# Where the modulation sums' weights and the rotary tables are made in a two-layer decoder trunk

## The chip, the cores and the metric

The kernel runs on one core of a Trainium2 chip. The metric is the device time of one execution in microseconds (us), given as the median of several runs. A core has TensorE (PE, the matrix multiplier, fed with weights by PEld), VectorE (DVE), ScalarE (ACT), GpSimd (POOL) and SyncE (SP). Each engine works through its own instructions in order; DMAs are issued from SP's and POOL's queues.

## What is computed

A trunk of two layers on 1024 tokens of width 1024, in float32:

```python
def reference(x, c, positions, ada_w, ada_b, norm_g, a_w_in, ...):
    cond = jax.nn.silu(c)
    cos, sin = rope_tables(positions)
    for l in range(DEPTH):
        ada = cond @ ada_w[l] + ada_b[l]
        sh1, sc1, g1, sh2, sc2, g2 = jnp.split(ada, 6, axis=-1)
        h = modulate(rmsnorm(x, norm_g[l, 0]), sh1, sc1)
        ...   # layer 0: mLSTM mixer; layer 1: latent attention on a shared K/V
        x = x + g1[:, None, :] * rmsnorm(y, norm_g[l, 1])
        h = modulate(rmsnorm(x, norm_g[l, 2]), sh2, sc2)
        y = sqrelu_mlp(h, mlp_w1[l], mlp_w2[l])
        x = x + g2[:, None, :] * rmsnorm(y, norm_g[l, 3])
    return x
```

Two things beside the large products matter here. The **modulation**: `cond @ ada_w[l]` is a vector times a 1024 x 6144 matrix for each layer, and `cond @ kv_ada_w` (1024 x 2048) one more for the shared K/V. The **rotary tables**: cosine and sine of position times 32 frequencies, for 1024 positions. They are needed only in layer 1.

```python
def rope_tables(positions):
    inv = ROPE_THETA ** (-jnp.arange(half, dtype=jnp.float32) / half)
    ang = positions.astype(jnp.float32)[..., None] * inv
    return jnp.cos(ang), jnp.sin(ang)
```

## The kernel before

**Products.** Every operand of a product is split into a high part (a cast on ACT, L238) and a low part (a subtraction on DVE, L239), and a product is three matmuls, L280 to L282. `wload` loads 512 KB of weights through SP (L260) into a buffer `raw`, of which there are four, and `wsplit` writes the two parts into two buffers `ws`, of which there are eight. Other buffers: 24 `k4` and eight `hd` of 128 x 1024 floats, six `tmc` and three `tmp` of 128 x 512, one `tma`.

**Halves and stages.** The tokens are worked in two halves of 512. In layer 0 each half goes through the gates (`gates_in`, `gates0`, L689 on: a chain of some twenty DVE and ACT instructions on eight partitions, whose results TensorE turns at L743), q, k and v, the weights within chunks (`intra0`), the chunks themselves (`chunks0`), the output gates (`og0`) and the output projection (`wout`). `split_o` (L797 to L801) multiplies the mixer's output by its gates and splits it. The MLP of layer 0 is then done in three sweeps, the first on the first half and the second on the second half with products of sums of blocks. In the second sweep a step loads a pair of 512 KB tiles (L1020), adds and subtracts them (L1026 to L1028), splits them (L1030, L1031, L238, L239) and stores one combination.

**Modulation.** `ada_chunk` makes 512 columns of a modulation vector: four loads of 512 KB (L377) into `raw`, eight multiply-adds on DVE into `tma` (L382, L384), and a transposition and a sum later on (L364, L366). The chunks are a generator, of which a step is taken here and there beside the products. In the first two sweeps what is left of them runs, and then `latent_weights`: six tiles of layer 1's latent weights are loaded into `raw` (L1563), summed with the shift on DVE (L1567, L1569), scaled on ACT (L1573), split with `wsplit`, and stored (L1578, L1580).

**Rotary tables.** `rope_tables` is drained as a whole ahead of the first gates. It runs on POOL on three `hd` buffers: a conversion, two scalings, seven reductions by parts of 2 pi (two instructions each, L2535 and L2536), a clamp; then two DVE instructions (L2539, L2540), two sines on ACT (L2541, L2542) and two stores. A sine needs another activation table than the exponentials around it.

**Order.** The program is written as generators that are woven by hand, but the final order of each engine's instructions is made by a planner, which runs over the whole program with modelled costs, takes ready instructions by priority (the order of the text, with those under `prompt` or `high_priority` 300 places earlier) and hands out the buffers. `paced` holds DVE instructions behind a given one. The start of the kernel is pinned in the order of the text.

Of the kernel before, what the change touches and what calls it, by code (L numbers as in the profile page):

```python
# [17 lines left out]
P = 128  # L18
# [64 lines left out]
def kernel(  # L83
# [286 lines left out]
    late = [False]  # L370

    def ada_chunk(w, c0, bias, dst):

        acc = tma()
        for q in range(4):
            r = raw().rearrange("p (a b) -> p a b", b=512)
            nc.sync.dma_start(r, wcols(w, c0, 512, 2 * q, 2))  # L377
            for kk in range(2):
                k = 2 * q + kk
                with paced():  # L380
                    if k == 0:
                        nc.vector.tensor_scalar(acc, r[:, kk], cond[:, 0:1], None, ALU.mult)  # L382
                    else:
                        nc.vector.scalar_tensor_tensor(  # L384
                            acc, r[:, kk], cond[:, k : k + 1], acc, ALU.mult, ALU.add
                        )
# [221 lines left out]
    def gates_in(hf):  # L608
# [6 lines left out]
        nc.gpsimd.memset(v7[:, :, 128:VE], 1.0)  # L615
        for t in range(4):
            v = k4()[:, : 7 * VE].rearrange("p (h e) -> p h e", e=VE)
            nc.gpsimd.memset(v[:, :, 128:VE], 1.0)
# [6 lines left out]
        nc.gpsimd.memset(g[:, :, :, 8:32], 0.0)  # L625
# [63 lines left out]
    def gates0(hf):  # L689
# [40 lines left out]
        nc.gpsimd.memset(RM.bitcast(F32), 0.0)  # L730
# [822 lines left out]
    def latent_weights():  # L1553
# [4 lines left out]
        for b, vs in enumerate(views):  # L1558
            A, sh = (Akv, kvada[:, 0:8]) if b < 3 else (Aq, adac(1, SH1))
            r_ = raw()  # L1560
            r = r_.rearrange("p (a b) -> p a b", b=P)
            for c0, v in vs:
                nc.sync.dma_start(r[:, :, c0 : c0 + v.shape[2]], v)  # L1563
            yield
            acc = tma()[:, :P]
            with paced():
                nc.vector.tensor_scalar(acc, r[:, 0], sh[:, 0:1], None, ALU.mult)  # L1567
                for k in range(1, KD):
                    nc.vector.scalar_tensor_tensor(  # L1569
                        acc, r[:, k], sh[:, k : k + 1], acc, ALU.mult, ALU.add  # L1570
                    )
            for k in range(KD):
                nc.scalar.activation(r[:, k], r[:, k], AF.Identity, scale=A[:, k : k + 1])  # L1573
            for i, t in enumerate(wsplit(r_, D)):
# [941 lines left out]
    def rope_tables():  # L2516
# [7 lines left out]
        d, a, kf = hd(), hd(), hd()  # L2524
        pi = d.bitcast(I32)
        nc.gpsimd.tensor_copy(d[:, 0:1], adac(0, SH1)[:, 7:8])
        nc.gpsimd.dma_start(pi, positions.to_broadcast([P, S]))
        nc.gpsimd.tensor_copy(a, pi)
        nc.gpsimd.tensor_scalar(a, a, inv, None, ALU.mult)
        yield  # L2530
        nc.gpsimd.tensor_scalar(kf, a, 1.0 / (2.0 * PI), MAGIC, ALU.mult, ALU.add)
        nc.gpsimd.tensor_scalar_add(kf, kf, -MAGIC)
        for part in TWO_PI_PARTS:
            yield
            nc.gpsimd.tensor_scalar(d, kf, -part, None, ALU.mult)  # L2535
            nc.gpsimd.tensor_add(a, a, d)  # L2536
        yield
        nc.gpsimd.tensor_scalar(a, a, 3.1415925, -3.1415925, ALU.min, ALU.max)
# [377 lines left out]
```

## Time and profile before

| | |
|---|---|
| median of 3 runs | 2339.2 us (2337.68 to 2341.8) |
| the profiled execution | 2336.3 us |
| its span, first to last instruction | 2334.1 us |
| PE busy | 2283.2 us, 98% |
| DVE busy | 1704.7 us, 73% |
| ACT busy | 1126.0 us, 48% |
| POOL busy | 146.3 us, 6% |
| read from and written to HBM | 343.65 and 98.57 MB, 189 GB/s over the span |

All that follows is read from one execution. In a view of waits a row has who waited (engine, tile, line), for whom, the total in us, how often, and the longest. In a view of stretches a row has the stretch and its length, the busy time of PE, PEld, DVE, ACT and POOL with the number of instructions, the clock that was granted to TensorE (1.00 is full), the mean busy share of the 16 DMA engines and GB/s. A row of the timeline begins with start and duration in us, and may end with the idle time before it and what ended it. Rows of groups give busy us and the mean ns of one.

### The profile page before, as it was taken

To read this page: it belongs to the slowest core of one execution; us is meant where nothing else is said; L and a number is where in the kernel's file an instruction comes from. 1 tells how busy PE (TensorE), PEld (TensorE's weight loads), DVE (VectorE), ACT (ScalarE), POOL (GpSimd) and SP (SyncE) were. 2 spreads that over 40 slices of the span, in tenths; PEclk is the share of its full clock that TensorE was granted. 3 is DMA by queue.
4 is the path that set the end of the run, shared out by engine and by line. 5 is a ranking of instruction groups with operands and counts; after the bars stand their busy time and mean duration, and the time that the engine had idled before them with its cause. 6 is when DMAs were issued, how large, how long until landed. Compare 5 with 4: busy or idle time off the path is not lost.

```text
span 2334.1 us, 32606 instructions
## 1 busy us (share of the span) xinstructions
PE 2283.2 (98%) x12042; PEld 1922.5 (82%) x12042; DVE 1704.7 (73%) x2749; ACT 1126.0 (48%) x1911; POOL 146.3 (6%) x231
## 2 busy tenths in 40 slices
PE   8899999999999999999999999999999999999998
PEld 6788798888877778778888778888888888989997
DVE  6776776879778777678774687765666488798776
ACT  4275334665335355544454464444444444655543
POOL 2700000000112220000000000000000000000000
PEclk9999999999999999999999999999999999999999
DMA  9452464657899888566686754874434452455432
GB/s 328 142 166 82 146 198 139 197 185 230 292 291 296 276 292 301 173 216 213 215 266 188 239 181 149 262 249 136 145 100 136 118 167 81 147 156 166 133 109 109
DMA packets 401103, 444.37 MB, mean 190 GB/s; under 512 B 26579, under 2 KB 288784, under 8 KB 400944
## 3 DMA queue, kind: packets, MB, share of 16 engines
q1 hardware_dynamic: 388000, 397.09, 53.7%
q0 software_dynamic: 12944, 45.20, 5.4%
q8 instruction: 95, 1.56, 0.3%
q14 instruction: 64, 0.52, 0.1%
HBM read 343.65 MB, written 98.57 MB: 189 GB/s over the span
## 4 chain that ended last, share of the span: by engine, by line
PE 77%; DVE 9%; DMA 8%; ACT 2%; issue 2%; SPq 1%; DVEq 0%; ACTq 0%
PE ps L280 13%; PE ps L282 12%; PE ps L281 12%; PE pm L280 9%; PE pm L281 9%; PE pm L282 8%; DMA raw<-in_mlp_w_dram 5%; PE pc L281 2%; PE pc L282 2%; PE pc L280 2%; DVE wl L239 1%; DMA raw<-in_a_w_in_dram 1%; PE pc L1969 1%; DVE k L247 1%; PE pm L1774 1%
## 5 line engine op out<-in xcount | busy, mean ns | idle before, releaser
L239 DVE TENSOR_TENSOR wl<-raw,wh 128x1024 fp32r<-128x1024 f32 (+5 forms) x323 | 382.6, 1187 | 210.2 <-ACT wh L238 185.3
L238 ACT CAST wh<-raw 128x1024 fp32r<-128x1024 f32 (+5 forms) x323 | 327.3, 1017 | 421.0 <-PE ps L281 164.7
L280 PE MATMUL ps<-k,wh 128*128 128x512 f32 (+1 forms) x1252 | 475.7, 380 | 5.6 <-DVE tmp L247 2.8
L282 PE MATMUL ps<-k,wl 128*128 128x512 f32 (+1 forms) x1252 | 467.9, 374 | 0.3 <-DVE wl L239 0.3
L281 PE MATMUL ps<-k,wh 128*128 128x512 f32 (+1 forms) x1252 | 467.7, 374 | 0.1
L280 PEld LDWEIGHTS ps<-k,wh 128*128 128x128 f32 x1252 | 235.9, 188 | 51.6 <-DVE tmp L247 3.6
L282 PEld LDWEIGHTS ps<-k,wl 128*128 128x128 f32 x1252 | 235.8, 188 | 42.9 <-DVE wl L239 0.9
L281 PEld LDWEIGHTS ps<-k,wh 128*128 128x128 f32 x1252 | 236.0, 188 | 41.9 <-issue 1.4
L247 DVE TENSOR_TENSOR k<-k,pm 128x512 f32<-128x512 f32 (+1 forms) x250 | 192.4, 801 | 62.7 <-PE pm L282 62.1
L280 PE MATMUL pm<-wh,hd 128*128 128x512 f32 x488 | 193.4, 396 | 2.6 <-ACT raw L1780 1.5
L282 PE MATMUL pm<-wh,hd 128*128 128x512 f32 x488 | 190.4, 390 | 0.0
L281 PE MATMUL pm<-wl,hd 128*128 128x512 f32 x488 | 190.4, 390 | 0.0
L384 DVE SCALAR_TENSOR_TENSOR tma<-raw,cond,tma 128x512 f32<-128x512 f32 x168 | 126.9, 755 | 23.3 <-DMA raw<-in_ada_w_dram 14.2
L280 PEld LDWEIGHTS pm<-wh,hd 128*128 128x128 f32 x488 | 91.7, 188 | 24.1 <-ACT raw L1780 4.0
L282 PEld LDWEIGHTS pm<-wh,hd 128*128 128x128 f32 x488 | 91.6, 188 | 19.9 <-DVE hd L494 0.5
L281 PEld LDWEIGHTS pm<-wl,hd 128*128 128x128 f32 x488 | 91.8, 188 | 18.4 <-issue 0.5
L281 PE MATMUL pm<-hd,wk 128*128 128x512 f32 x256 | 100.0, 391 | 1.7 <-DVE hd L494 1.7
L280 PE MATMUL pm<-hd,wk 128*128 128x512 f32 x256 | 100.8, 394 | 0.6 <-ACT hd L493 0.6
L1780 ACT ACTIVATE raw<-pm,sm 128x128 f32<-128x128 f32 (+3 forms) x64 | 47.5, 743 | 110.8 <-DVE sm L1779 107.2
L280 PE MATMUL pm<-hd,wh 128*128 128x512 f32 x256 | 99.5, 390 | 0.9 <-DVE tma L384 0.9
L282 PE MATMUL pm<-hd,wl 128*128 128x512 f32 x256 | 99.7, 390 | 0.5 <-DVE wl L239 0.5
L282 PE MATMUL pm<-hd,wk 128*128 128x512 f32 x256 | 99.8, 390 | 0.0
(494 smaller groups left out, 4857.5 us busy)
## 6 DMA issues: line engine op xcount, KB each, us to landing
raw<-in_mlp_w_dram SPq DMA_DIRECT2D x176, 512.0 KB, 4.6
raw<-in_ada_w_dram SPq DMA_DIRECT2D x80, 512.0 KB, 4.8
raw<-in_mlp_w_dram SPq DMA_DIRECT2D x128, 256.0 KB, 4.6
raw<-in_a_w_in_dram SPq DMA_DIRECT2D x44, 512.0 KB, 4.5
lo<-wl POOLq DMA_DIRECT2D x32, 512.0 KB, 7.0
wk<-lo SPq DMA_DIRECT2D x64, 256.0 KB, 3.8
xs<-k SPq DMA_DIRECT2D x40, 256.0 KB, 4.4
raw<-in_a_w_out_dram SPq DMA_DIRECT2D x16, 512.0 KB, 4.5
```

The source lines that it names most:

```text
L238: nc.scalar.copy(hi[:, :n], r[:, :n])
L239: i = nc.vector.tensor_sub(lo[:, :n], r[:, :n], hi[:, :n].bitcast(F32))
L247: return f(*a, **k)
L280: nc.tensor.matmul(o, lh, rh, start=start, stop=False)
L281: nc.tensor.matmul(o, lh, rl, start=False, stop=False)
L282: pe_last[0] = nc.tensor.matmul(o, ll, rh, start=False, stop=stop)
L384: nc.vector.scalar_tensor_tensor(acc, r[:, kk], cond[:, k : k + 1], acc, ALU.mult, ALU.add)
L1774: nc.tensor.matmul(o[:, :w], qh, kh, start=False, stop=True)
L1780: nc.scalar.activation(pr[:, :n], f, AF.Exp, bias=m, scale=SCALE, accum_out=l)
L1969: nc.tensor.transpose(pt[:, ts(2 * e + i, P)], u.prs[i][:, ts(b + e, P)], ident)
```

## The change

The diff has two parts.

Part 1 moves `rope_tables`. It is no longer drained ahead of the first gates, but taken two steps at a time beside the eight output gates of the second half. Its POOL instructions become DVE instructions, and a reduction by a part of 2 pi is one instruction in place of two. Its buffers are `k4` in place of `hd`. The memsets on POOL in `gates_in` and `gates0` go to DVE too.

Part 2 adds a flag `apart`, which is set while the first two sweeps are woven. With it `ada_chunk` loads each 512 KB as two DMAs of 256 KB into two `tmc` in place of one `raw`. `latent_weights` always loads its tiles into two `tmc`, and splits them in two halves into two `ws`.

```diff
-    late = [False]
+    late, apart = [False], [False]
...
-            r = raw().rearrange("p (a b) -> p a b", b=512)
-            nc.sync.dma_start(r, wcols(w, c0, 512, 2 * q, 2))
+            if apart[0]:
+                r = [tmc(), tmc()]
+                for kk in range(2):
+                    nc.sync.dma_start(r[kk], w[ts(2 * q + kk, P), c0 : c0 + 512])
+            else:
+                r = raw().rearrange("p (a b) -> p a b", b=512)
+                nc.sync.dma_start(r, wcols(w, c0, 512, 2 * q, 2))
+                r = [r[:, 0], r[:, 1]]
...
-        nc.gpsimd.memset(v7[:, :, 128:VE], 1.0)
+        nc.vector.memset(v7[:, :, 128:VE], 1.0)
         for t in range(4):
...
-            nc.gpsimd.memset(v[:, :, 128:VE], 1.0)
+            nc.vector.memset(v[:, :, 128:VE], 1.0)
...
-        nc.gpsimd.memset(g[:, :, :, 8:32], 0.0)
+        nc.vector.memset(g[:, :, :, 8:32], 0.0)
...
-        nc.gpsimd.memset(RM.bitcast(F32), 0.0)
+        nc.vector.memset(RM.bitcast(F32), 0.0)
...
-            r_ = raw()
-            r = r_.rearrange("p (a b) -> p a b", b=P)
+            r = [tmc(), tmc()]
+            cols_ = lambda t: t.rearrange("p (a b) -> p a b", b=P)
             for c0, v in vs:
-                nc.sync.dma_start(r[:, :, c0 : c0 + v.shape[2]], v)
+                for i in range(2):
+                    nc.sync.dma_start(cols_(r[i])[:, :, c0 : c0 + v.shape[2]], v[:, ts(i, 4)])
...
+            of = lambda k: r[k // 4][:, ts(k % 4, P)]
...
             for k in range(KD):
-                nc.scalar.activation(r[:, k], r[:, k], AF.Identity, scale=A[:, k : k + 1])
-            for i, t in enumerate(wsplit(r_, D)):
+                nc.scalar.activation(of(k), of(k), AF.Identity, scale=A[:, k : k + 1])
+            for i in range(2):
+                nc.scalar.copy(hi[:, ts(i, 512)], r[i])
+                nc.vector.tensor_sub(lo[:, ts(i, 512)], r[i], hi[:, ts(i, 512)].bitcast(F32))
+            for i, t in enumerate((hi, lo)):
...
-        d, a, kf = hd(), hd(), hd()
+        d, a, kf = k4()[:,:1024],k4()[:,:1024],k4()[:,:1024]
         pi = d.bitcast(I32)
-        nc.gpsimd.tensor_copy(d[:, 0:1], adac(0, SH1)[:, 7:8])
         nc.gpsimd.dma_start(pi, positions.to_broadcast([P, S]))
-        nc.gpsimd.tensor_copy(a, pi)
-        nc.gpsimd.tensor_scalar(a, a, inv, None, ALU.mult)
+        nc.vector.tensor_copy(a, pi)
+        nc.vector.tensor_scalar(a, a, inv, None, ALU.mult)
...
         for part in TWO_PI_PARTS:
             yield
-            nc.gpsimd.tensor_scalar(d, kf, -part, None, ALU.mult)
-            nc.gpsimd.tensor_add(a, a, d)
+            nc.vector.scalar_tensor_tensor(a, kf, -part, a, ALU.mult, ALU.add)
...
-    drain(rope_tables())
     drain(with_bg(gates_in(hfs[0]), bgs, 1))
...
     so = split_o(hfs[1])
+    tables = rope_tables()
     for k, _ in enumerate(og0(hfs[1], k4v)):
         if k % 2:
             prompt(next)(so)
         next(bgs)
+        for _ in range(2):
+            next(tables, None)
         if k < 7:
             next(p0)
...
+    apart[0] = True
     two_streams(f0, behind(bg_latent(), 5))
+    apart[0] = False
     rope_perm()
```

18 lines of the change are left out of this document (10 added, 8 removed).

## The prediction

> **What bounds the kernel now.** I read the totals of the page first, then the waits of TensorE, then the stretches in which they lie.
>
> ```profile
> span 2334.1 us, 32606 instructions
> PE 2283.2 (98%) x12042; PEld 1922.5 (82%) x12042; DVE 1704.7 (73%) x2749; ACT 1126.0 (48%) x1911; POOL 146.3 (6%) x231
> ```
>
> TensorE (PE) is busy 2283.2 of 2334.1 us, so an edit that leaves its instructions alone can win at most the 50.9 us in which it stands, and the time it runs at a lower clock. Two stretches that the change touches hold a good part of that. This is the longest wait of TensorE from 78 to 142 us (the gates of the first half of the tokens), and the busy times there (columns: PE, weight load, DVE, ACT, POOL, clock, DMA share, GB/s):
>
> ```profile
> PE pc L743 <- DVE tmc L712: 6.1, 1, 6.1
> ...
> 78.00:142.00 64.00, 55.30 (x388) 49.02 (x387) 55.62 (x79) 31.64 (x70) 28.02 (x14) 0.92 0.53 165
> 98.20:105.00 6.80, 6.60 (x42) 6.37 (x42) 6.56 (x11) 0.52 (x1) 4.27 (x3) 0.77 0.00 0
> 105.00:115.00 10.00, 9.06 (x59) 7.61 (x59) 9.04 (x18) 2.97 (x7) 0.00 (x0) 0.83 0.35 102
> ```
>
> TensorE stands 64 - 55.3 = 8.7 us, 6.1 of them in one wait. The clock costs more: 6.8 us at 0.77 and 10 us at 0.83 lose 0.23 x 6.8 + 0.17 x 10 = 3.3 us, of which I count 2.2, since TensorE also stands there. So 10.9 us can be had. The same two views for the first two sweeps of the first MLP:
>
> ```profile
> PE ps L282 <- DVE wv L1031: 3.8, 4, 1.3
> PE ps L280 <- ACT wv L1030: 3.6, 2, 2.1
> PE ps L280 <- DVE tmp L247: 2.8, 2, 2.1
> ...
> 549.00:860.00 311.00, 298.28 (x1305) 241.18 (x1304) 245.32 (x352) 127.57 (x200) 59.96 (x87) 0.99 0.88 283
> 820.00:840.00 20.00, 19.38 (x78) 15.51 (x78) 15.29 (x20) 8.30 (x13) 4.21 (x7) 0.91 0.97 306
> ```
>
> Here TensorE stands 311 - 298.3 = 12.7 us, and 20 us at a clock of 0.91 lose 1.8 more: 14.5 us can be had. The three waits shown, 10.2 us, all lie in sweep 2.
>
> **Part 1a, the tables leave POOL.** The chain of the gates on VectorE (DVE), once beside POOL's tables and once, for the second half of the tokens, with POOL idle:
>
> ```profile
> 82.68 2.60 DVE L696 TENSOR_SCALAR tmc<-tmc,cols 8x512 f32<-8x512 f32 x1
> 88.22 2.76 DVE L704 SCALAR_TENSOR_TENSOR tmc<-tmc,tmc 8x512 f32<-8x512 f32 x1
> 93.17 4.26 DVE L709 TENSOR_TENSOR_SCAN tmc<-ones,tmc 8x128 f32<-8x128 f32 x4
> 98.18 0.47 DVE L715 TENSOR_TENSOR_SCAN tmc<-ones,mcol,tmc 8x128 f32<-8x128 f32 x1
> ...
> 241.88 0.47 DVE L696 TENSOR_SCALAR tmc<-tmc,cols 8x512 f32<-8x512 f32 x1
> 244.76 0.68 DVE L704 SCALAR_TENSOR_TENSOR tmc<-tmc,tmc 8x512 f32<-8x512 f32 x1
> ...
> L2535 POOL TENSOR_SCALAR hd<-hd 128x1024 f32<-128x1024 f32 x7 | 20.8, 2965 | 0.5
> ```
>
> The same instruction on eight partitions takes 0.47 us without POOL and 2.60 us with it, 0.68 and 2.76: it waits for a good part of one POOL instruction (2.97 us). L696 and L704 lose 2.13 + 2.08 = 4.2 us, and the four scans, at the 0.47 us of a lone one, lose 4.26 - 1.88 = 2.4. That makes 6.6 us ahead of L712, for which TensorE waited 6.1 us: without POOL, L712 is done before TensorE asks. The wait goes and with it most of the lowered clock that follows it. POOL's own time is no gain, since nothing waits for it. Late next is the load of the v weights, whose buffers are freed by DVE in the same crowded stretch and which then need a DMA, a cast and a subtraction; so I don't take all of the 10.9 us but **8.5**. Bounds: 4 (only part of the large wait goes) and 10.9.
>
> The memsets that go to DVE are 14 small ones. Each costs the path nothing unless its tile is still held; DVE stands in order, so one that waits holds back the weight splits behind it. With the twelve half-width casts and subtractions of the latents' weights, in place of six whole ones, I put **0.5 us** (0 to 1.5).
>
> **Part 1b, the tables' new place.** What they cost DVE and ACT, and what is there beside the second output gates (395 to 444 us) and behind them:
>
> ```profile
> L2539 DVE SCALAR_TENSOR_TENSOR hd<-hd 128x1024 f32<-128x1024 f32 x1 | 1.2, 1214 | 0.0
> L2540 DVE TENSOR_SCALAR hd<-hd 128x1024 f32<-128x1024 f32 x1 | 0.7, 678 | 0.0
> ...
> L2541 ACT ACT_TABLE_LOAD x1 | 1.3, 1283 | 0.0
> L2541 ACT ACTIVATE hd<-hd 128x1024 f32<-128x1024 f32 x1 | 1.1, 1063 | 0.0
> ...
> 395.00:444.00 49.00, 49.00 (x218) 40.17 (x217) 39.09 (x54) 32.59 (x50) 0.79 (x8) 1.00 0.69 222
> 444.00:480.00 36.00, 36.00 (x159) 29.45 (x158) 25.89 (x34) 20.59 (x31) 0.00 (x0) 1.00 0.51 166
> ...
> 443.53 1.22 DVE L801 TENSOR_TENSOR k<-hd,k 128x1024 fp32r<-128x1024 f32 x1 [0.52 <-ACT k L800]
> ...
> ACT wh L238 <- PE pm L281: 10.1, 5, 3.2
> ```
>
> DVE: the copy, the five one-input passes and the moved one, 7 x 0.68; the seven reductions and the moved one, 8 x 1.21: 14.4 us. ACT: two sines and up to four table loads (it alternates with the gates' exponentials, as it does now with others), 2 x 1.06 + 4 x 1.28 = 7.2 us. DVE has 9.9 us free up to 444 and 10.1 us from there to 480: it fits only if some 5 us slide behind the gates. What slides is what was traced late and has no priority: the tables, and the first residual. Weight splits and the split of the gated output are pushed ahead, and the splits have cover: ACT waits up to 3.2 us for TensorE to free their buffers. Cover is thin in one place: the last split of the output ends at 444.75, when the projection that reads it has begun. I take a loss of **1.0 us**. Bounds: nothing, and 9.3 us: if all 14.4 us go ahead of that split, less the 7 us that DVE stands in front of it, it is 7.4 us late, and a lowered clock after it costs another 1.9 by the 2.2 above. A gain here is excluded, since TensorE stands nowhere in this window. The tables need three of the 24 large buffers where the gated output's split takes eight; those of the gates come free as the split advances, so I count no wait for them. What else is issued (positions, the two stores) goes to POOL's queue, which is empty there.
>
> **Part 2, small buffers.** Now the modulation sums and latents' weights share the four `raw` buffers with the MLP's weights:
>
> ```profile
> SPq L1020 <- DVE wl L239: 46.0, 14, 9.3
> ...
> DVE k L1026 <- DMA raw<-in_mlp_w_dram: 32.7, 14, 4.3
> ...
> 795.79 0.45 SPq L1563 DMA_DIRECT2D raw<-in_b_w_q_a_dram  x1
> ...
> 789.89 0.50 PE L280 MATMUL ps<-k,wv 128*128 128x512 f32 x1 [1.44 <-ACT wv L1030]
> ...
> 820.53 0.50 PE L280 MATMUL ps<-k,wv 128*128 128x512 f32 x1 [2.13 <-ACT wv L1030]
> ...
> 819.88 0.60 ACT L1030 CAST wv<-raw 128x512 fp32r<-128x512 f32 x1
> ...
> 817.18 1.18 ACT L1573 ACTIVATE raw<-raw,mods 128x128 f32<-128x128 f32 x3 [0.90 <-DVE tma L1569]
> ```
>
> SP waits 46.0 us, 14 times, for DVE's splits to free a `raw` before it can issue sweep 2's weight loads (L1020), and DVE then stands 32.7 us until they land. A latents' tile holds one of the four from its load at 795.79 until it is scaled at 817.18, and TensorE's stall of 820.53 follows; that of 789.89 stands one such tile earlier. With four buffers for the weights alone, one of a pair of loads can go a round earlier. But two things remain. The pair's sum reads the second tile, and its buffer still comes free in the same burst of splits; and the row at 817.18 shows the cast behind eight scalings on ACT that wait for DVE's sums, which no buffer changes. So I take about half of the 14.5 us, **7.0**, between 0 and 14.5.
>
> The added waits: each half load waits for a small buffer, and behind it on SP stand the weight loads, as they do today behind waits for `raw`. The issues themselves: 27 loads of the sums and 7 of the latents become 68, each 0.37 us on SP, 12.6 us over 311, hidden behind the 46.0 us that SP waits.
>
> ```profile
> L377 SPq DMA_DIRECT2D raw<-in_ada_w_dram x16: 367/368/442, 603.2 to 676.0; - x16
> L377 SPq DMA_DIRECT2D raw<-in_kv_ada_w_dram x11: 367/368/531, 549.1 to 593.8; - x11
> ...
> L1563 SPq DMA_DIRECT2D raw<-in_kv_w_a_dram x4: 368/1168/2238, 691.6 to 738.2; - x4
> L1563 SPq DMA_DIRECT2D raw<-in_b_w_q_a_dram x3: 447/472/520, 765.5 to 825.1; - x3
> ...
> raw<-in_mlp_w_dram SPq DMA_DIRECT2D x176, 512.0 KB, 4.6
> ...
> raw<-in_mlp_w_dram SPq DMA_DIRECT2D x128, 256.0 KB, 4.6
> ```
>
> **Sum.** -8.5 + 0.5 + 1.0 - 7.0 = -14.0 us. The profiled execution took 2336.3 us, 2.2 above its span; the median of the runs is 2339.2, 2.9 higher. I take the difference from the median: **2325 us**, and 2316 to 2333 for this case alone.
>
> **Rivals.** *Sweeps unchanged*: the second buffer of the pair and the scalings on ACT decide, and part 2 gives nothing: 2339.2 - 7.0 = 2332. For it speaks the row at 817.18; against it that the stalls come with the latents' tiles. Chance 0.17.
>
> *The tables take it back*: 9.3 us lost beside the gates, -8.5 + 0.5 + 9.3 - 7.0 = -5.7: 2333.5. For it DVE's 39.09 of 49 us; against it the priority of the splits. Chance 0.11.
>
> *Slower, the halved loads fill the DMA engines*: both sizes land in 4.6 us in the rows above. The stage moves 311 us x 283 GB/s = 88 MB, some 168 loads of 512 KB, in 0.88 x 311 = 274 us of all engines, 1.63 us each; 37 us are free. If a half takes as long as a whole, 34 more take 55 us, 18 more than is free, and the sweeps become bound by transfers: 2339.2 - 7.0 + 18 = 2350. It costs something from 37 / 34 = 1.1 us for each added load, and more than part 1 gains from 1.3. Against it: the rows of a half are as long as those of a whole (512 columns), so the packets are the same. Chance 0.10. The Trainium skill (DMA: Bandwidth & Descriptors, Bandwidth) speaks for this rival: it wants loads of 1 MiB and more for three quarters of the peak. That smaller loads don't land sooner here (4.6 and 4.6 us) agrees with it.
>
> *All of it* (10.9 + 14.5 with nothing lost): 2314, chance 0.05. The forecast has 0.57.
>
> **How the numbers follow.** About 0.2% (4.7 us) is what a measurement of this kernel can tell from no change, so faster begins below 2334.5. The forecast, the full gain, most of the first rival and half of the second lie there: 0.78. Within 0.2% lie the rest of these: 0.10. Slower: the third rival, and a little for a new order of the instructions, which the planner makes anew for the whole kernel: 0.12. For 8 in 10 the range takes in the forecast's own, the full gain and the first two rivals with some spread: 2311 to 2338.
>
> **What would show it.** Right: L696 and L704 at about 0.5 and 0.7 us in the first gates, no wait for L712, the clock at 1.0 from 98 to 115 us; no standing of TensorE from 395 to 480; fewer waits on L1030, L1031 and L247 in sweep 2, and SP's waits before L1020 shorter. Wrong: waits for L801 or the first residual near 444; stalls in sweep 2 as before beside an early L1020; a DMA share near 1.0 there. The whole would be wrong if the new order opened waits far from the change, after 900 us, where I counted none.

## The result, and the profile after

The changed kernel takes **2322.6 us** (median of 4 runs, 2319.4 to 2324.0), the kernel before 2340.5 us beside it (4 runs, 2337.7 to 2341.8): a ratio of 0.9923, 95% interval 0.9906 to 0.9940. The forecast was 2325, in a range of 2311 to 2338. The profiled execution of the changed kernel took 2324.0 us, 12.3 less than that of before. The medians differ by 17.9, since that execution of before lay 4.2 below its median and this one 1.5 above.

In the changed kernel lines from L384 up to the latents' weights bear numbers 6 higher, those behind it 13 higher: L696, L704, L709, L712, L1020, L1030 and L1031 are now L702, L710, L715, L718, L1026, L1036 and L1037. L377 is L382 where a sum goes through `raw` and L379 where it goes through `tmc`; L1563 is L1570 and L1573 is L1583.

The totals of the page:

```profile
span 2322.2 us, 32704 instructions
...
PE 2280.8 (98%) x12042; PEld 1921.8 (83%) x12042; DVE 1702.5 (73%) x2782; ACT 1129.4 (49%) x1919; POOL 90.7 (4%) x196
```

TensorE now stands 41.4 us in place of 50.9, and ran the same 12042 matmuls in 2.4 us less, at a mean clock of 0.998 in place of 0.996.

**The first gates.** The timeline of DVE, the waits of TensorE from 70 to 145 us (there is no other), and the busy times there (columns as before):

```profile
82.81 0.47 DVE L702 TENSOR_SCALAR tmc<-tmc,cols 8x512 f32<-8x512 f32 x1
...
85.14 0.68 DVE L710 SCALAR_TENSOR_TENSOR tmc<-tmc,tmc 8x512 f32<-8x512 f32 x1
...
87.66 1.36 DVE L715 TENSOR_TENSOR_SCAN tmc<-ones,tmc 8x128 f32<-8x128 f32 x4
```

```profile
PE pc L791 <- ACT tmc L775: 0.5, 1, 0.5
```

```profile
78.00:145.00 67.00, 66.47 (x482) 59.58 (x480) 53.36 (x111) 32.15 (x80) 0.00 (x0) 1.00 0.60 179
98.00:105.00 7.00, 6.54 (x56) 5.66 (x55) 5.58 (x10) 2.25 (x7) 0.00 (x0) 1.00 0.54 154
```

The instructions that took 2.60, 2.76 and 4.26 us take 0.47, 0.68 and 1.36. The wait of 6.1 us is gone, 0.5 us of standing is left of 8.7, and the clock is at 1.00 where it was 0.77.

**The tables' new place.** The reductions on DVE, and the busy times of the second output gates and of what follows:

```profile
L2547 DVE SCALAR_TENSOR_TENSOR k<-k,k x7: 1215/1217/1219, 399.3 to 414.0; 128x1024 f32<-128x1024 f32 x7
```

```profile
392.00:441.00 49.00, 49.00 (x218) 40.22 (x217) 46.37 (x59) 36.02 (x49) 0.55 (x1) 1.00 0.66 211
441.00:480.00 39.00, 39.00 (x172) 31.96 (x171) 32.56 (x43) 28.37 (x40) 1.48 (x10) 1.00 0.64 200
```

DVE is busy 46.4 of 49 us, and TensorE doesn't stand at all, there or up to 480.

**The first two sweeps.** The longest waits of TensorE, the busy times of the same 311 us, and SP's waits ahead of sweep 2's pairs of loads:

```profile
PE ps L280 <- ACT wv L1036: 1.4, 1, 1.4
PE ps L280 <- DVE tmp L247: 1.1, 2, 0.5
PE pc L282 <- DVE wl L239: 1.0, 2, 0.5
```

```profile
549.00:860.00 311.00, 306.72 (x1357) 250.15 (x1356) 253.49 (x368) 135.32 (x215) 63.10 (x96) 1.00 0.89 294
```

```profile
SPq L1026 <- DVE wv L1037: 44.4, 13, 7.3
...
SPq L1026 <- DVE wl L239: 20.3, 12, 5.0
```

TensorE is busy 8.4 us more of the same stretch (306.72 against 298.28), and the rate rose from 283 to 294 GB/s at nearly the same DMA share (0.88, 0.89). SP's two waits were 33.1 and 46.0 us in before.

**What wasn't forecast.** TensorE's waits from 200 to 400 us, the first of them in the timeline, and the busy times behind it:

```profile
PE ps L280 <- ACT wh L238: 1.5, 1, 1.5
PE pc L890 <- DVE tmc L864: 1.1, 1, 1.1
PE ps L282 <- DVE wl L239: 0.5, 1, 0.5
```

```profile
269.75 0.50 PE L280 MATMUL ps<-k,wh 128*128 128x512 f32 x1 [1.49 <-ACT wh L238]
```

```profile
270.00:280.00 10.00, 9.47 (x43) 7.68 (x43) 6.97 (x10) 3.43 (x6) 0.00 (x0) 0.83 0.77 220
271.00:274.00 3.00, 3.00 (x7) 2.42 (x8) 1.87 (x3) 0.09 (x1) 0.00 (x0) 0.50 0.91 273
```

The kernel before had 0.6 us of waits there. The clock of 0.83 is the mean of some three us at half clock (the second row) and the rest at full. This 3.1 us of standing and the lowered clock lie in the second half's gates and chunks, which the prediction didn't price.

To place all this, each kernel's span is cut at seven events that all kernels share: the first turning of the gates by TensorE (L640), the first and the last output-gate exponential of the first half (L682), the first one of the second half, the first store of sweep 1 (L1003), the last of sweep 2 (L1053), and the last load of the latents' weights (L1605; lines of before). In us, with what TensorE stands in brackets where it matters; "again" is e12, a second profiled execution of the changed kernel:

| kernel | start | first gates | outputs 1 | second half | outputs 2 | sweeps | MLP, rest of it | rest | span |
|---|---|---|---|---|---|---|---|---|---|
| before | 72.2 | 83.7 (8.7) | 63.4 | 180.2 (0.6) | 86.8 | 391.6 (12.8) | 530.5 | 925.7 | 2334.1 |
| changed | 72.4 | 72.6 (0.5) | 63.5 | 184.1 (3.1) | 86.8 | 382.2 (4.3) | 534.2 | 926.4 | 2322.2 |
| changed, again | 73.9 | 72.6 (0.5) | 63.5 | 183.7 (2.6) | 86.7 | 380.4 (2.5) | 532.3 | 926.2 | 2319.3 |
| e1_part1 | 75.5 | 72.7 (0.5) | 63.4 | 182.2 (2.6) | 86.8 | 388.5 (11.0) | 534.4 | 929.2 | 2332.7 |
| e2_part2 | 71.9 | 83.5 (9.0) | 63.4 | 180.1 (0.4) | 86.8 | 378.5 (1.6) | 533.4 | 927.1 | 2324.7 |
| e3_halves | 73.9 | 81.2 (6.2) | 63.5 | 178.9 (0) | 86.8 | 385.5 (8.8) | 532.9 | 925.1 | 2327.8 |
| e4_dve_early | 77.7 | 74.7 (5.6) | 63.4 | 181.3 (1.7) | 86.7 | 389.1 (9.8) | 533.0 | 927.8 | 2333.7 |
| e5_null | 73.8 | 81.4 (6.3) | 63.5 | 180.0 (0.4) | 86.8 | 390.4 (12.4) | 532.3 | 927.8 | 2336.0 |
| e6_sums_only | 73.6 | 83.4 (8.3) | 63.5 | 180.3 (0.6) | 86.7 | 385.2 (7.5) | 531.1 | 927.2 | 2331.0 |
| e7_latents_only | 72.7 | 83.3 (8.3) | 63.4 | 180.1 (0.5) | 86.7 | 385.4 (6.0) | 533.1 | 928.2 | 2332.9 |
| e8_pool_late | 73.1 | 72.7 (0.5) | 63.4 | 188.4 (5.6) | 87.3 | 389.4 (11.5) | 532.2 | 928.2 | 2334.7 |
| e9_sums_apart | 74.3 | 72.7 (0.5) | 63.4 | 185.7 (4.5) | 86.7 | 378.6 (1.9) | 532.6 | 926.1 | 2320.1 |
| e10_memsets_pool | 73.5 | 72.4 (0) | 63.5 | 180.9 (1.3) | 86.7 | 377.8 (1.6) | 532.5 | 927.6 | 2314.9 |
| e11_after_null | 73.3 | 72.6 (0.5) | 63.4 | 182.4 (2.8) | 86.8 | 379.7 (3.0) | 532.8 | 924.8 | 2315.8 |

### The profile page after: what moved, and what is told of

Its sections match the earlier page's. It is cut to its first block, busy times and chain, and to the rows that moved or that the text cites. A ratio compares the mean times of both kernels' runs of the same rounds, so it can differ in the third digit from the quotient of the medians.

```text
span 2322.2 us, 32704 instructions
## 1 busy us (share of the span) xinstructions
PE 2280.8 (98%) x12042; PEld 1921.8 (83%) x12042; DVE 1702.5 (73%) x2782; ACT 1129.4 (49%) x1919; POOL 90.7 (4%) x196
## 4 chain that ended last, share of the span: by engine, by line
PE 78%; DMA 8%; DVE 8%; issue 2%; ACT 2%; SPq 1%; POOL 0%; DVEq 0%; ACTq 0%; POOLq 0%
PE ps L280 13%; PE ps L282 13%; PE ps L281 13%; PE pm L280 8%; PE pm L281 8%; PE pm L282 8%; DMA raw<-in_mlp_w_dram 4%; PE pc L281 2%; PE pc L280 2%; PE pc L282 2%; DVE wl L239 1%; DVE k L247 1%; PE pc L1982 1%; DMA raw<-s 1%; PE pm L1787 1%
## 5 line engine op out<-in xcount | busy, mean ns | idle before, releaser
L238 ACT CAST wh<-raw 128x1024 fp32r<-128x1024 f32 (+2 forms) x317 | 321.4, 1016 | 430.5 <-PE ps L281 178.0
L239 DVE TENSOR_TENSOR wl<-raw,wh 128x1024 fp32r<-128x1024 f32 (+2 forms) x317 | 375.0, 1185 | 197.4 <-ACT wh L238 172.8
L281 PEld LDWEIGHTS ps<-k,wh 128*128 128x128 f32 x1252 | 236.6, 189 | 41.4 <-issue 1.4
L281 PEld LDWEIGHTS pm<-wl,hd 128*128 128x128 f32 x488 | 91.8, 188 | 18.3 <-issue 0.5
L390 DVE SCALAR_TENSOR_TENSOR tma<-raw,cond,tma 128x512 f32<-128x512 f32 x120 | 89.5, 746 | 17.6 <-DMA raw<-in_ada_w_dram 8.4
L281 PE MATMUL pm<-hd,wk 128*128 128x512 f32 x256 | 100.1, 391 | 1.7 <-DVE hd L500 1.7
L280 PE MATMUL pm<-hd,wk 128*128 128x512 f32 x256 | 100.9, 394 | 0.6 <-ACT hd L499 0.6
L280 PE MATMUL pm<-hd,wh 128*128 128x512 f32 x256 | 99.5, 390 | 1.1 <-ACT hd L499 0.8
L281 PE MATMUL pm<-hd,wh 128*128 128x512 f32 x256 | 99.7, 390 | 0.2 <-DVE hd L500 0.2
```

The lines of the kernel that those rows point to most:

```text
L238: nc.scalar.copy(hi[:, :n], r[:, :n])
L239: i = nc.vector.tensor_sub(lo[:, :n], r[:, :n], hi[:, :n].bitcast(F32))
L280: nc.tensor.matmul(o, lh, rh, start=start, stop=False)
L281: nc.tensor.matmul(o, lh, rl, start=False, stop=False)
L390: nc.vector.scalar_tensor_tensor(acc, r[kk], cond[:, k : k + 1], acc, ALU.mult, ALU.add)
```

## The experiments

The theory to test was the prediction's own: part 1 gains in the first gates because POOL no longer stretches DVE there, and part 2 gains in the sweeps because background tiles no longer hold the MLP's `raw`. The rivals: the halving of the loads does what the buffers seem to do, or the planner's new order does it.

The programs were also set side by side, engine by engine. Part 2 alone moves no instruction of TensorE and none of any engine ahead of the sweeps, though it does give DVE, ACT and SP a new order within them; part 1 moves instructions of TensorE only ahead of the sweeps. Behind the sweeps no row of TensorE stands elsewhere in the changed kernel. So before, e2, e5, e6 and e7 are five executions of one order up to the sweeps, and the changed kernel, e1, e11 and e12 four of another. Their spread is the measure of what one execution can show: first gates 81.4 to 83.7 and 72.6 to 72.7, second half 180.0 to 180.3 and 182.2 to 184.1.

### Each part alone: e1_part1 and e2_part2

e1 is the changed kernel with the sums and the latents' tiles as before; e2 is the kernel before with them as in the diff.

```diff
 e1, against the changed kernel
-    apart[0] = True
     two_streams(f0, behind(bg_latent(), 5))
-    apart[0] = False
...
-            r = [tmc(), tmc()]
+            r_ = raw()
 e2, against the kernel before
+    apart[0] = True
     two_streams(f0, behind(bg_latent(), 5))
+    apart[0] = False
...
-            r_ = raw()
+            r = [tmc(), tmc()]
```

> Part 1 alone: tables on VectorE beside the second output gates, memsets on VectorE, the modulation sums and latents' weights in the large buffers as before. Theory (POOL slowed VectorE's chain of gates; the sweeps are a matter of buffers): the first output gate's exponential (155.9 us before, 145.0 after) comes at 145.0 +- 0.5, the second output gates (399.5, 392.6) at about 392.6, the first block of sweep 1 (its first store at 486.3, 479.4) at about 479.4, and the two sweeps keep their 391.6 us (first store of sweep 1 to last store of sweep 2; 382.2 after), so that some 7 us of the gain remain: about 2332 to 2334. Rival (a new order made by the planner gives the gain, in whatever part): the stages differ from both kernels, and the sweeps are shorter here too.

> Part 2 alone: the modulation sums and latents' weights through six small buffers in the first two sweeps, tables on POOL at the start as before. Theory (buffers): first output gate at 155.9 +- 0.5 as before, with TensorE's wait of 6.1 us for the gates; from the first store of sweep 1 to the last store of sweep 2 382 +- 2 us in place of 391.6; about 9 us less in all, some 2331. Rival (the parts need each other: the sweeps are faster only because VectorE or POOL come to them less loaded): the sweeps keep more than 388 us.

Measured: e1 2331.3 us (6 runs), ratio 0.9967 (0.9954 to 0.9979); e2 2325.1 us (4 runs), ratio 0.9942 (0.9928 to 0.9957), before 2338.5. The forecast gave each part 7.0 us (-8.5 + 0.5 + 1.0, and -7.0); part 1 has that, and part 2 is the larger: 13.3 us of time against 7.1. The table shows where: e1 has the whole gain of the first gates (83.7 to 72.7) and loses 2.0 in the second half; e2 gains 13.1 us in the sweeps and leaves the stages ahead of them as they were. The numbers of the expectations were missed in places: e1's first output gate came at 148.2 us and not at 145.0, since its start took 75.5 us, and its sweeps took 388.5 and not 391.6; e2's took 378.5, less than the 380 to 384 expected. Both rivals fall: e2's sweeps are short without part 1, and e1's gain lies in the gates, its sweeps being only 1.9 to 3.1 us shorter than in two executions of before (e5 is the other). The waits in e2's sweeps, longest first:

```profile
PE pc L282 <- DVE wl L239: 0.9, 2, 0.5
PE pm L280 <- ACT hd L499: 0.5, 1, 0.5
PE ps L280 <- ACT wv L1036: 0.3, 1, 0.3
```

Of the 10.2 us in the three rows of before, 0.3 is left.

### Halving without the buffers, and a null: e3_halves and e5_null

e3 keeps `raw` and only loads each sum's and each latents' tile as two halves of 256 KB. e5 is the kernel before with one memset that does no work that counts, written at the latents' weights and meant to make the planner order the kernel anew.

```diff
 e3, against the kernel before
-            nc.sync.dma_start(r, wcols(w, c0, 512, 2 * q, 2))
+            for kk in range(2):
+                nc.sync.dma_start(r[:, kk], w[ts(2 * q + kk, P), c0 : c0 + 512])
...
-                nc.sync.dma_start(r[:, :, c0 : c0 + v.shape[2]], v)
+                for i in range(2):
+                    nc.sync.dma_start(r[:, ts(i, 4), c0 : c0 + v.shape[2]], v[:, ts(i, 4)])
 e5, against the kernel before
         Aq = gain(5, NG(1, 0), adac(1, SC1))
+        nc.vector.memset(lbias[:, 0:1], 0.0)
```

> The kernel before with only the loads of the modulation sums (all of them) and of the latents' weights halved: two DMAs of 256 KB (the latents' too) into the same large buffer. Theory (the packets are the same, only the buffers count): the sweeps keep 391.6 +- 2 us, DMA share there 0.88 as before, total 2337 to 2342. Rival of the prediction (a half load costs the engines as much as a whole): the share rises towards 1.0 and the sweeps take 18 us more, about 2355. Other rival (the halving itself brings the gain, since a half lands earlier): the sweeps fall towards 382.

> Control: the kernel before with one superfluous memset of one column on VectorE ahead of the latents' weights. It changes nothing that the prediction speaks of, but the planner orders everything behind it anew. Theory (the gain of part 2 is a matter of buffers, that of the later stages a matter of order): TensorE's standing in the two sweeps stays between 11 and 13 us (12.75 before, 11.0 with part 1 alone), and the later stages (last store of sweep 2 to the end, 1456.2 before, 1458 to 1464 in the other four) come out some us longer than before's, since its order is only one of several. Rival (any new order gives the sweeps' gain): standing below 8 us.

e3 took 2329.6 us in one run; its sweeps 385.5 us, 6.1 less than before. Its waits there and its busy times:

```profile
PE ps L280 <- ACT wv L1031: 4.3, 2, 2.3
PE ps L282 <- DVE wv L1032: 2.7, 4, 1.0
...
549.00:860.00 311.00, 302.20 (x1330) 246.18 (x1329) 248.76 (x357) 131.55 (x206) 62.65 (x90) 0.99 0.89 288
```

So the expectation failed: the sweeps didn't keep their 391.6 us. By this one run halving alone brings about half of part 2's gain, and not where the buffers bring theirs: the waits for the pairs' cast and subtraction (L1031 and L1032, L1030 and L1031 in before) are still 7.0 us. They were 7.4. With the sums alone in small buffers these waits are 3.6 us, with the latents' alone 1.4 (e6 and e7, below), with both 0.3. The rival that a half lands earlier has something for it here: in the sweeps e3's halves of the sums landed in 4.5 and 5.0 us (median, from the two tensors), the whole loads of before in 5.6 and 5.5. Nor do the halves fill the DMA engines: the share is 0.89 against 0.88, at 288 GB/s against 283.

e5 took 2336.5 us (8 runs), ratio 0.9995 (0.9983 to 1.0006). It did not do what it was meant to: the planner put the memset among DVE's first instructions, at 2.2 us of the trace, and left every other row of every engine where it was. So it says nothing of a new order. That rival is answered for TensorE, which e2 doesn't move; for the order of DVE, ACT and SP within the sweeps, which is new in e2, e3, e6 and e7, it stays open. As it is, e5 is a second execution of the kernel before: first gates 81.4 and not 83.7, sweeps 390.4 and not 391.6, and behind the sweeps 1460.1 us in place of 1456.2. The profiled execution of before, on which the prediction was built, was a lucky one at its end.

### Which tiles: e6_sums_only and e7_latents_only

Both on the kernel before: in e6 only the sums go through `tmc`, in e7 only the latents' tiles.

```diff
 e6, against e2
-            r = [tmc(), tmc()]
+            r_ = raw()
 e7, against e2
-    apart[0] = True
     two_streams(f0, behind(bg_latent(), 5))
-    apart[0] = False
```

> The kernel before with the modulation sums alone through halved loads into small buffers in the first two sweeps; the latents' weights stay in a large one. Theory: what stands at the sums' loads (L364, the first product of sweep 2, L247: some 4 us of 12.75) goes, and the latents' rounds keep their stalls on L1030 and L1031 (7.4 us and the lowered clock): standing 7 to 9 us in the sweeps, 385 +- 2 us for them. Rival (all of it is the prefetch of the sums): standing below 4.

> The kernel before with the latents' weights alone through small buffers. Theory: the stalls on the casts and subtractions of sweep 2's weights (7.4 us with a lowered clock) go, those at the sums' loads stay: standing 3 to 6 us in the sweeps, 381 to 385 us. The prediction's doubt (the casts stand behind the scalings on ACT, and no buffer changes that): the stalls on L1030 and L1031 stay, standing 10 or more.

One run each: 2332.8 and 2334.7 us. The sweeps are 6.4 us shorter with the sums alone and 6.2 with the latents alone, 13.1 with both: the two add up. The waits of TensorE in the sweeps and SP's ahead of the pairs, e6 first:

```profile
PE ps L280 <- ACT wv L1036: 2.2, 1, 2.2
...
SPq L1026 <- DVE wl L239: 59.1, 16, 10.6
SPq L1026 <- DVE wv L1037: 39.1, 14, 7.0
```

```profile
PE ps L282 <- DVE wv L1037: 1.4, 2, 1.0
...
SPq L1026 <- DVE wv L1037: 42.7, 12, 7.0
...
SPq L1026 <- DVE wl L239: 15.1, 11, 5.0
```

With the latents out of `raw`, SP waits 57.8 us before the pairs' loads; with them in it 98.2 (before: 46.0 + 33.1). SP's waits alone don't set the time: e6 has more of them than before and shorter sweeps. The wait for the cast L1036 has gone in e7. But the order on ACT has changed with the buffers. In before, from the second of the six tiles on, the cast stands behind all eight scalings of a tile and the tile's own cast (the prediction's rows at 817.18 and 819.88); in e7, as in e2 and the changed kernel, it runs between them:

```profile
808.35 1.56 ACT L1583 ACTIVATE tmc<-tmc,mods 128x128 f32<-128x128 f32 x4 [2.83 <-DVE tma L1575]
...
810.47 0.40 ACT L1583 ACTIVATE tmc<-tmc,mods 128x128 f32<-128x128 f32 x1
810.77 0.60 ACT L1036 CAST wv<-raw 128x512 fp32r<-128x512 f32 x1
...
812.24 0.98 ACT L1583 ACTIVATE tmc<-tmc,mods 128x128 f32<-128x128 f32 x3
```

So e7 doesn't tell the buffers from the order on ACT: either could have taken this stall, and no run holds one of the two still.

### Engine or place: e4_dve_early and e8_pool_late

Both are e1 with one half of part 1 undone. In e4 the tables run on DVE, but ahead of the first gates as before. In e8 they run at the new place, but on POOL.

```diff
 e4, against e1
+    drain(rope_tables())
     drain(with_bg(gates_in(hfs[0]), bgs, 1))
...
-    tables = rope_tables()
...
-        for _ in range(2):
-            next(tables, None)
 e8, against e1 (so for each of the tables' instructions)
-        nc.vector.tensor_scalar(a, a, inv, None, ALU.mult)
+        nc.gpsimd.tensor_scalar(a, a, inv, None, ALU.mult)
...
-            nc.vector.scalar_tensor_tensor(a, kf, -part, a, ALU.mult, ALU.add)
+            nc.gpsimd.tensor_scalar(d, kf, -part, None, ALU.mult)
+            nc.gpsimd.tensor_add(a, a, d)
```

> Part 1 with the tables on VectorE but at their old place, drained ahead of the first gates; part 2 left out. Tells the engine from the place. Theory (what cost TensorE 10.9 us was VectorE being late with the gates, by POOL's contention): 14.4 us of table work on VectorE in the stretch where it is busy 55.6 of 64 us must be done somewhere before 145; the planner can put it behind the gates, so L696 and L704 take about 0.5 and 0.7 us, and the first output gate comes between 145 and 156, nearer 148. Rival (the place alone matters): the first output gate stays at 155 or later, with TensorE waiting for the gates again.

> Part 1 with the tables' instructions still on POOL, at the new place beside the second output gates; part 2 left out, memsets on VectorE. Tells the place from the engine. Theory (POOL slows only what runs beside it, and beside the second output gates the weights are split ahead): the first output gate comes as early as with part 1 (72.7 us behind the first turn of the gates, 83.7 before); VectorE's two-input instructions take longer from 395 to 460 us, and TensorE stands there 0 to 3 us. Rival (contention costs the same wherever it is): TensorE stands 6 us or more there, and the gain of the gates is lost again.

One run each: 2335.5 and 2336.5 us. e8's first gates take 72.7 us, as e1's: to take the tables out of the place is enough, whatever engine they are on. e4's chain has short instructions too, but the tables' stand between them: its first output gate comes at 152.4 us of the span, e1's at 148.2, that of before at 155.9. That is 3.5 of e1's 7.7 us. Against all executions (155.2 to 157.0 in before's order, 145.0 to 148.2 in the new one) it is rather a third. In the table a part of what is lost shows in e4's start, 77.7 us, in which most of the tables' instructions run (from 66.8 us on). So the engine alone is worth a third to a half of the gain, less than the theory's "nearer 148", and the rival's 155 or later didn't come either:

```profile
85.16 0.47 DVE L702 TENSOR_SCALAR tmc<-tmc,cols 8x512 f32<-8x512 f32 x1
85.55 1.20 DVE L2543 SCALAR_TENSOR_TENSOR k<-k 128x1024 f32<-128x1024 f32 x1
...
89.17 0.68 DVE L710 SCALAR_TENSOR_TENSOR tmc<-tmc,tmc 8x512 f32<-8x512 f32 x1
```

e8 then loses elsewhere. Its planner drew most of the tables' work forward from the output gates to the chunks, so that what POOL costs beside the output gates wasn't tested as meant. The busy times of its chunks, the largest of the tables' groups on POOL and the wait there:

```profile
346.00:392.00 46.00, 42.00 (x230) 34.67 (x229) 34.87 (x66) 14.50 (x34) 35.16 (x15) 0.93 0.35 103
```

```profile
L2540 POOL TENSOR_SCALAR k<-k 128x1024 f32<-128x1024 f32 x7 | 20.1, 2866 | 0.6
```

```profile
PE pc L890 <- DVE tmc L864: 4.0, 1, 4.0
```

And the same small instruction of DVE in the chain ahead of L864, in e8 and in e1:

```profile
367.30 2.12 DVE L859 SCALAR_TENSOR_TENSOR sm<-sm 128x4 f32<-128x4 f32 x1
```

```profile
369.19 0.16 DVE L859 SCALAR_TENSOR_TENSOR sm<-sm 128x4 f32<-128x4 f32 x1
```

POOL is busy 35.2 of these 46 us, and TensorE stands 4.0 of them in one wait for DVE, where it waits 0.9 to 1.1 us with the tables on DVE beside the output gates. It is the loss of the first gates once more at another place.

### The second half's loss: e9_sums_apart, e10_memsets_pool, e11_after_null, e12_after_again

These four start from the changed kernel. e9 lets the sums use `tmc` from the second half's gates on; e10 puts the memsets of `gates_in` and `gates0` back on POOL; e11 adds e5's memset, and as there it moved no other row; e12 is the changed kernel unaltered.

```diff
 e9
     drain(gates_in(hfs[1]))
+    apart[0] = True
...
     drain(bg0)
+    apart[0] = False
 e10 (and so for the other three)
-        nc.vector.memset(RM.bitcast(F32), 0.0)
+        nc.gpsimd.memset(RM.bitcast(F32), 0.0)
 e11
+        nc.vector.memset(lbias[:, 0:1], 0.0)
```

> The changed kernel, but the modulation sums load through the small buffers also beside the second half's gates and output (from the second half's gates to its last chunk), where they still go through raw. Theory A: the changed kernel loses 3.9 us there because a sum's tiles hold raw, so that SP stands 20.6 us before the load of the next v weights and TensorE then stands 1.5 us and loses 1.7 us of clock: the stage from the first half's last to the second half's first output-gate exponential falls from 184.1 to 180 to 181 us, SP's wait before L260 for the sums goes from 20.6 us to under 5, and the time is 2318 to 2320. Theory B: the loss comes from DVE alone, which is fuller there since the memsets and the gates' chain moved: the stage stays at 183 to 185 us though SP waits less, and the time stays at 2322. Theory C: six small buffers, which the gates use as well, become scarce there: the gates wait for them and the stage is over 185 us, the time 2325 or more.

> The changed kernel with its fourteen small memsets (the ones of the v tiles, the gates' zeros, RM) back on POOL. Theory A: the memsets cost nothing on either engine: every stage within 0.7 us of the changed kernel, the second half's stage at 184 us, the time 2322. Theory B: the memsets on DVE hold the weight splits back by what I put at 0.5 us, or more: the first gates or the second half's stage are 0.5 to 3 us shorter, 2319 to 2321.5. Theory C: the memsets themselves, beside DVE, are part of what part 1 took away: the first gates are 1 us or more longer than 72.6.

> The changed kernel with one more memset on DVE, of a column that is written again before it is read, placed in the latents' weights: it does no work that counts, but the order of everything behind the first sweep is made anew, while the order ahead of it stays as it is. Theory A: what the changed kernel gives back behind the sweeps (+3.7 and +0.7 us against before) is the luck of an order: the third MLP part and the rest sum to something else by 2 us or more (1460.6 us in the changed kernel, 1456.2 before), while the first gates stay at 72.6 and the second half's stage at 184.1 within 0.7. Theory B: it belongs to the change: the sum stays at 1460 to 1461.5 us. The sweeps stay at 380 to 384 us under both.

> The changed kernel once more, unaltered, on another chip. It has the same instructions in the same order as its first run, and from the first MLP on nearly the order of the kernel with the memsets on POOL, whose sweeps took 377.8 us against 382.2. Theory A: what the memsets on DVE cost in the second half's stage is the same every time: TensorE stands 2.5 to 3.1 us there and waits 1.1 to 1.5 us for the cast L238, the stage takes 182 to 184.5 us (memsets on POOL: 1.25 us, no such wait, 180.9 us); the time is 0.992 to 0.993 of before. Theory B: both are chance of one execution: the standing is under 2 us, the stage 180 to 181.5 us, the time near 0.991 of before as with the memsets on POOL. For the sweeps: if one execution differs from another by some us, this one lies between 378 and 381 us; if the 4.4 us belong to the memsets, at 382 again.

**e9**: 2322.3 us (5 runs), ratio 0.9939 (0.9926 to 0.9953). Theory A is half right. The stall near 270 us and its lowered clock are gone, but the stage is longer, 185.7 us, because another wait has come, for a sum itself. The wait, and the busy times of the ten us in which it lies:

```profile
PE pc L364 <- DVE tma L390: 3.7, 1, 3.7
```

```profile
320.00:330.00 10.00, 6.33 (x29) 5.38 (x28) 7.81 (x22) 1.55 (x4) 0.00 (x0) 0.83 0.30 88
```

So without the sums' hold on `raw` that stall doesn't come, and to free it at this place only moves it: C's number for the stage came true, but not by gates that wait. The hold alone doesn't make the stall, though. SP stands as long there in before, without it (before first, then the changed kernel):

```profile
SPq L260 <- DVE tma L384: 28.3, 6, 20.9
```

```profile
SPq L260 <- DVE tma L390: 29.3, 7, 20.6
```

**e10**: 2317.0 us (4 runs), ratio 0.9912 (0.9898 to 0.9925). The second half takes 180.9 us. Its longest wait of TensorE from 145 to 395 us, and under it the two longest of e12:

```profile
PE pc L890 <- DVE tmc L864: 0.9, 1, 0.9
```

```profile
PE ps L280 <- ACT wh L238: 1.2, 1, 1.2
PE pc L890 <- DVE tmc L864: 0.9, 1, 0.9
```

The wait for the cast L238 is there in the changed kernel's two executions, e1, e4, e8 and e11 (1.1 to 1.5 us each), which have these memsets on DVE and the sums in `raw`. It is absent in e10, which differs from the changed kernel by the memsets alone, and in before, e2, e6 and e7, which have them on POOL. **e12** took 2319.2 us (5 runs), ratio 0.9924 (0.9911 to 0.9938), with the second half at 183.7 us again. So these memsets on DVE cost 1.3 to 3.2 us in this stage: Theory B of e10 and A of e12, at the lower end with the 182.2 and 182.4 us of e1 and e11. The two ends differ by the clock: behind this wait it was lowered in the changed kernel's two executions (0.83 over ten us) and stayed at 1.00 in e1 and e11.

The traces show most of the way from the memsets to the stall. This is the load that the cast waits for, in before, the changed kernel and e10, where the stage begins at 219.3, 208.5 and 209.4 us:

```profile
273.85 0.37 SPq L260 DMA_DIRECT2D raw<-in_a_w_in_dram  x1
```

```profile
264.39 0.37 SPq L260 DMA_DIRECT2D raw<-in_a_w_in_dram  x1
```

```profile
263.92 0.37 SPq L260 DMA_DIRECT2D raw<-in_a_w_in_dram  x1
```

It is issued 54.5 to 54.6 us into the stage in before, e2, e5, e6, e7 and e10, which have the memsets on POOL, and 55.9 to 56.0 us into it in the changed kernel, e1, e4, e8, e11 and e12, which have them on DVE. Its `raw` comes free with a sum on DVE that stands behind the gates' chain, and that chain ends 1.4 us later there. A cast that comes 1.4 us later is a wait of 1.1 to 1.5 us. What delays the chain isn't shown: the fourteen memsets are small (the largest takes 0.48 us), and some of DVE's and TensorE's instructions stand in another order in e10. By the times alone e10 and the changed kernel are not told apart: their intervals overlap.

**e11**: 2317.3 us (4 runs), ratio 0.9919 (0.9904 to 0.9934). Its expectation rested on a new order behind the first sweep, and there was none. So its 1457.6 us behind the sweeps are one more execution of the changed kernel, beside 1460.6 and, in e12, 1458.5. Theory A's 2 us were met by chance of the execution.

e10 has the lowest time of all that ran.

## Why the prediction came out

| step | forecast | first execution | e12 | e11 |
|---|---|---|---|---|
| 1a, the first gates | -8.5 (-4 to -10.9) | -11.1 | -11.1 | -11.1 |
| memsets and half splits (second half) | +0.5 (0 to 1.5) | +3.9 | +3.5 | +2.2 |
| 1b, the tables' place | +1.0 (0 to 9.3) | 0.0 | -0.1 | 0.0 |
| 2, the sweeps | -7.0 (0 to -14.5) | -9.4 | -11.2 | -11.9 |
| behind the sweeps | 0 | +4.4 | +2.3 | +1.4 |
| start and outputs 1 | 0 | +0.3 | +1.8 | +1.1 |
| sum, of the span | -14.0 | -11.9 | -14.8 | -18.3 |

All three are taken against the one execution of before that the prediction used. Against e5 the first column's first gates would be -8.8 and what lies behind the sweeps +0.5.

**1a was right in its mechanism and undersized.** The standing of 8.7 us fell to 0.5 and the clock came back. The forecast kept 2.4 us back for a late load of the v weights behind the wait; no such wait followed in the first gates. By the five executions of before's order (83.1 us in the mean) and the four of the new one (72.6) the gain is 10.5 us, near the bound of 10.9. e8 shows that POOL at this place is the cause, whatever engine the tables run on elsewhere.

**The memsets were mis-sized.** The prediction priced them on the path they stand on, at 0.5 us with a bound of 1.5, and never looked at the second half's gates, where they make a chain late; behind it stands a sum that holds a `raw`, and behind that a load with no margin. By the same nine executions the stage is 3.0 us longer (180.1 to 183.1), of which e10 gives 2.2 back; what is left lies in the wait L890 for L864, 0.9 us in e10 too. This is the one bound that the runs broke. The prediction's last paragraph looked for such a wait only after 900 us.

**1b was right, at its lower bound.** DVE is 46.4 of 49 us busy, the output gates and the projection take 86.8 us in both kernels, and TensorE never stands. ACT loads its tables six times (422.65 to 443.38 us), where the forecast counted four, at 1.28 us each, and that costs nothing either. What slides, as argued, is the tables: their last DVE instruction runs at 437 us. The rival in which they take the gain back has fallen.

**Part 2 was right in sign and undersized, by a doubt that didn't come true.** The forecast took half of 14.5 us, because the second tile's buffer still comes free late and because the cast stands behind eight scalings, "which no buffer changes". e2 gave 13.1 of the 14.5. The order on ACT, which the forecast held fixed, changed with the buffers: from the second tile on, the cast stands behind five to seven scalings in place of all eight. Whether it would have been late behind all eight is open. The rival *sweeps unchanged* has fallen by the times. In the changed kernel's three executions the gain is 9.4, 11.2 and 11.9 us, in e10, with all but the same order there, 13.8. Why one execution keeps 4.3 us of standing where another keeps 1.6 is open. A little of it comes back directly behind the sweeps, as said below.

**The halved loads did not fill the DMA engines.** Each half was priced at a whole load's 1.63 us of all engines. Measured: 34 more loads at shares of 0.89 and 0.90, 294 and 295 GB/s in the changed kernel and e2. The share rose no faster than the rate, so by these, as an estimate, a half took about half as long of the engines as a whole. The forecast compared landings over the whole kernel, of other weights. In the sweeps the sums' loads land in 5.6 and 5.5 us in before, their halves in 5.7 and 5.6 in the changed kernel and in 4.5 and 5.0 in e3. The Trainium skill (DMA: Bandwidth & Descriptors, Bandwidth) wants loads of 1 MiB and more for three quarters of the peak; between 512 and 256 KB, at this share, no run here shows a loss of rate. That agrees with the argument against this rival, that the packets stay the same.

**Behind the sweeps** the forecast had 0. The time of these 1460 us is too uncertain to tell more from it: the 13 other executions took 1457.6 to 1463.6 us, and e5, with none of the change, 1460.1. It is the 1456.2 of the execution used that stands out. But part 2 does cost something there. In the first 30 us behind the last store of sweep 2, in before and the changed kernel:

```profile
877.90:907.90 30.00, 30.00 (x135) 24.82 (x134) 18.89 (x22) 14.87 (x22) 1.59 (x3) 1.00 0.87 324
```

```profile
861.60:891.60 30.00, 28.12 (x122) 22.39 (x121) 18.61 (x22) 13.75 (x20) 1.57 (x3) 1.00 0.89 321
```

TensorE stands there 1.3 to 1.9 us in all seven kernels that have the latents' tiles in `tmc`, and not at all in the seven that have them in `raw`, though its instructions are the same. So of what part 2 wins in the sweeps this much is given back at once.

So the forecast's 2325 came near 2322.6 partly by luck, by errors of both signs: some 2 to 2.6, 1.0 and 2.4 to 4.9 us too little gain in its three large terms, against 2.5 too little loss by the memsets' stage and the 1.3 to 1.9 us behind the sweeps. The parts agree with the whole: by the ratios part 1 alone is worth 7.7 us and part 2 alone 13.6, together 21.3; the changed kernel has 18.0 of it and e10 20.6.

## What to carry to other kernels

When a background stream shares prefetch buffers with the main one, look at the wait of the queue that issues both: a tile that is consumed late holds back every load behind it, and the stall can show far from the tile, as a wait for a cast or a subtraction of a quite different weight. Such an edit may also change the order on the other engines, so look at that before naming the buffer as the cause. Before moving small instructions to another engine, look for every place where they run, not only for the one that the change is about: here fourteen memsets gave back about a fifth of what the tables' move had won. And when a stall goes, the clock that it had lowered comes back too: count both in full unless a named wait stands behind. But the same stall lowers the clock in one execution and not in the next, so take the sum from more than one execution, for a stage far from the change can differ by 4 us by itself.

## What the hardware showed that wasn't expected

- One wait of 1.5 us (changed kernel, 269.75) was followed by some three us at half clock, which makes the ten us from 270 a mean of 0.83; the ten us of e9 that hold its wait of 3.7 us have the same 0.83. The clock costs 0.17 x 10 = 1.7 us, as much as the short stall itself. But it doesn't always fall: behind the same wait (1.1 and 1.4 us) it stayed at 1.00 in e1 and e11.
- How well a stage repeats with the same order depends on the stage: outputs 1 and 2 within 0.1 us, the second half of before within 0.3 and its first gates within 2.3, the changed kernel's sweeps only within 2.5 (382.2, 380.4, 379.7) and its start within 1.5.
- POOL's contention reaches whatever DVE chain it stands beside: in the first gates of before a wait of 6.1 us, beside the chunks in e8 one of 4.0, with a DVE instruction of 0.16 us stretched to 2.12.
